# All four projections of the attention layer by seven half-size products, with half the buffers

## The chip, the cores and the metric

The kernel runs on one NeuronCore of one Trainium2 chip. The metric is the device time of one execution in microseconds (us), the median of several runs. In the profile the engines are PE (TensorE, matrix products), DVE (VectorE), ACT (ScalarE), POOL (GpSimd) and SP (SyncE, which here only issues transfers). Each has its own instruction stream, worked off in order; they meet through semaphores.

## The reference, cut to what matters

Two layers over 640 rows of 1024 numbers: 512 rows of a prompt and 8 x 16 rows of samples. Layer 0 is a gated MLP, layer 1 an attention. All data are float32.

```
proj = h @ w_in                       # layer 1: (640 x 1024) @ (1024 x 8208)
q, k, v, z = proj[:, 0:2048], proj[:, 2048:4096], proj[:, 4096:6144], proj[:, 6144:8192]   # 16 heads of 128
logf = log_sigmoid(proj[:, 8192:] + b_f)
# prompt, per head:  p = softmax(q k^T / sqrt(128) + c_i - c_j, causal),  c = cumsum(logf)
# samples: the same over 256 cached rows and the 16 new ones (cache_fox_k, cache_fox_v)
op = (p @ v * silu(z)) @ w_out
x = x + rms_norm(op);  x = x + sigmoid(x @ ple_w_gate) * (p @ ple_w_proj)
```

k and v of the new rows are outputs too.

## The kernel before

**Precision.** Every large float32 product is three products of rounded halves: `split` (lines 270 to 273) has ScalarE write the rounded half `hi` and VectorE the rest `lo = src - hi`, and `mm3` (lines 256 to 260) multiplies hi by hi, hi by lo and lo by hi into the same PSUM bank. A weight is fetched into RAW (three buffers of 512 KB), split into W, and then used; `prefetch` does this as far ahead as W has free places, and `fetch` issues the transfers.

**Layer 0** already makes its u and z projections by `seven_products` (line 533): the four quarters of a product of 256 x 1024 by 1024 x 640 come from seven products of half the size in each direction (Winograd's form of Strassen's scheme) instead of eight. It needs sums of the quarters of the weight, which POOL makes from RAW into a tile `sf` (`left_operands`, line 200), and sums of the quarters of h, which `right_operands` makes once on VectorE and ScalarE into a tile `tb` (lines 409 to 417). Each product covers 4 steps of 128 over the contraction, so 12 matmuls of 320 columns; ScalarE and VectorE add the results up (lines 540 to 555).

**Layer 1** runs over eight pairs of heads. For each pair, `project_v`, `project_k`, `project_q` and `project_z` make 256 columns of the projection. k, q and z come out with heads on partitions (`channel_steps`, line 316): for each of 2 heads and 8 steps three matmuls of 384 columns (`mm3`), one of 512 (line 324) and one of 256 (line 325). v comes out with rows on partitions: for 5 row tiles and 8 steps one matmul of 512 (line 867) and one of 256 columns (line 868). While pair p+1 is projected, the attention of pair p is worked in between: the prompt's scores in four blocks per head, and the samples in two groups of four. Keys of the cache are loaded with the transposition half done and turned by VectorE (line 1018).

**What sets the order.** `interleave` takes a generator of projection steps, each of which yields its time in us, and a list of (time, piece): a piece of the attention is issued when the steps' sum has passed its time. A scheduler then puts the instructions of all engines in a final order by a timeline of its own. All transfers stand in SP's stream, in order (line 119). PSUM has eight banks: 0 to 3 for projections, 4 to 6 for the attention in turn, 7 for the prompt's output.

Of the kernel before, what the change touches and what calls it, by code (L numbers as in the profile page):

```python
# [24 lines left out]
P = 128  # L25
# [32 lines left out]
def hybrid_trunk(tc, x_prompt, x_sample, ck, cv, clf, p_prompt, p_sample, norm_pre, norm_post,  # L58
# [4 lines left out]
    N_SMALL = 288  # L63
    N_R1 = 17664
# [89 lines left out]
    joined = set()  # L154
    for p in range(8):
        for part in (2, 1, 0, 3):
            for kk in range(2):
                if part == 2:
                    joined.add(len(units))
                u_rows(f_win[0], kk * 512, part * E + p * 256, 4, 256)  # L160
# [6 lines left out]
    for i in range(len(units)):  # L167
        if not S0 <= i < S1:
# [4 lines left out]
    n0 = S1 + 16 + 2 + 8  # L173
    few = range(n0, n0 + 64 + 12)
# [28 lines left out]
    def prefetch(upto, i0=0):  # L203

        while len(place) < min(upto, len(items)):
# [64 lines left out]
    def split(hi, lo, src):  # L270

        nc.scalar.activation(out=hi, in_=src, func=AF.Copy)  # L272
        nc.vector.tensor_tensor(out=lo, in0=src, in1=f(hi), op=ALU.subtract)  # L273
# [41 lines left out]

    h_both = A.rearrange("p (z k n) -> p z k n", z=2, k=8)

    def channel_steps(ws, hh, banks):

        out = [bank(banks), bank(banks)]  # L320
        for k in range(8):
            w = [z[:, k % 4, hh * P:(hh + 1) * P] for z in ws[k // 4]]
            mm3(out[0][:, :SA], w, h_at(k, 0, SA), k == 0, k == 7)
            nc.tensor.matmul(out[1].rearrange("p (z n) -> p z n", z=2), w[0], h_both[:, :, k, SA:], start=k == 0, stop=False)  # L324
            nc.tensor.matmul(out[1][:, :TOK - SA], w[1], h_hi[:, k, SA:], start=False, stop=k == 7)  # L325
            yield 0.88
        return out
# [79 lines left out]
    b11, b12, b21, b22, t_a, t_b = (r1(10240 + z * 1280, 1280).rearrange("p (k n) -> p k n", k=4) for z in (0, 1, 2, 3, 4, 0))  # L407

    def right_operands():

# [3 lines left out]
        for o, a, b, dst in ((t_a, b12, b11, 0), (t_b, b22, t_a, 1), (b21, b21, t_b, 2), (b12, b22, b12, None)):  # L414
            nc.vector.tensor_tensor(out=o, in0=a, in1=b, op=ALU.subtract)
# [755 lines left out]
```

## Time and profile before

| | |
|---|---|
| median of 3 runs | 1315.37 us (1315.07 to 1315.51) |
| the profiled execution: its own time | 1315.17 us |
| its span, first to last instruction | 1313.4 us |
| PE busy | 1304.7 us (99%) |
| DVE, ACT, POOL busy | 794.1, 553.1, 136.1 us |
| layer 0, u and z projections | about 150 to 345 us of the span |
| layer 1, its projections begin | at about 531 us |
| layer 1, pairs 1 to 6 beside the attention of 0 to 5 | about 603 to 1042 us, 73 us each |
| output product and tail | from about 1110 us |

A row of an engine's timeline gives start and duration of an instruction. Matmuls are pipelined: a row's duration is longer than the distance to the next row, and it is the distance that costs time. PEld is PE's loading of weights, which runs beside the products. In a row of instruction groups the last number ahead of the bar's second half is the mean duration in ns.

### The profile page before, as it was taken

To read this page: it belongs to the slowest core of one execution; us is meant where nothing else is said; L and a number is where in the kernel's file an instruction comes from. 1 tells how busy PE (TensorE), PEld (TensorE's weight loads), DVE (VectorE), ACT (ScalarE), POOL (GpSimd) and SP (SyncE) were. 2 spreads that over 40 slices of the span, in tenths; PEclk is the share of its full clock that TensorE was granted. 3 is DMA by queue.
4 is the path that set the end of the run, shared out by engine and by line. 5 is a ranking of instruction groups with operands and counts; after the bars stand their busy time and mean duration, and the time that the engine had idled before them with its cause. 6 is when DMAs were issued, how large, how long until landed. Compare 5 with 4: busy or idle time off the path is not lost.

```text
span 1313.4 us, 20355 instructions
## 1 busy us (share of the span) xinstructions
PE 1304.7 (99%) x7683; PEld 1152.3 (88%) x7683; DVE 794.1 (60%) x1671; ACT 553.1 (42%) x1074; POOL 136.1 (10%) x144
## 2 busy tenths in 40 slices
PE   8999999999999999999999999999999999999998
PEld 6888999999988888888999889898988988888887
DVE  7744999999844455644555554556555566554543
ACT  5334555444535343533433334333434344435431
POOL 1012454543000000000000000000000000000100
PEclk8999999999999999999999999999999999999999
DMA  6432333232424213589676665788557687343211
GB/s 227 132 108 67 120 118 121 86 104 73 129 94 149 79 49 113 167 135 149 152 194 151 155 160 148 165 150 171 132 150 163 149 213 235 113 132 132 66 56 57
DMA packets 300053, 172.79 MB, mean 132 GB/s; under 512 B 188785, under 2 KB 269473, under 8 KB 299954
## 3 DMA queue, kind: packets, MB, share of 16 engines
q1 hardware_dynamic: 299810, 171.23, 49.3%
q8 instruction: 60, 0.98, 0.3%
q14 instruction: 39, 0.32, 0.1%
q10 hardware_dynamic: 144, 0.26, 0.1%
HBM read 149.86 MB, written 21.59 MB: 131 GB/s over the span
## 4 chain that ended last, share of the span: by engine, by line
PE 95%; DVE 3%; DMA 1%; issue 1%; ACT 0%; SPq 0%; POOL 0%; DVEq 0%
PE pb L258 22%; PE pb L260 22%; PE pb L259 22%; PE pb L324 7%; PE pb L867 6%; PE pb L325 3%; PE pb L868 3%; PE pb L986 3%; PE pb L979 1%; PE pb L1040 1%; PE pb L1066 1%; PE pb L296 1%; DVE W L273 1%; PE pb L571 1%; PE pb L1063 1%
## 5 line engine op out<-in xcount | busy, mean ns | idle before, releaser
L273 DVE TENSOR_TENSOR W<-RAW,W 128x1024 fp32r<-128x1024 f32 (+1 forms) x156 | 193.5, 1242 | 170.8 <-ACT W L272 136.5
L272 ACT ACTIVATE W<-RAW 128x1024 fp32r<-128x1024 f32 (+1 forms) x156 | 161.0, 1033 | 151.0 <-PE pb L260 47.5
L258 PE MATMUL pb<-A,W 128*128 128x384 f32 (+1 forms) x640 | 221.8, 347 | 0.0
L260 PE MATMUL pb<-A,W 128*128 128x384 f32 (+1 forms) x640 | 208.7, 326 | 0.0
L259 PE MATMUL pb<-A,W 128*128 128x384 f32 (+1 forms) x640 | 208.3, 325 | 0.0
L258 PE MATMUL pb<-W,A 128*128 128x512 f32 x520 | 205.0, 395 | 2.3 <-ACT A L272 2.3
L259 PE MATMUL pb<-W,A 128*128 128x512 f32 x520 | 203.7, 392 | 0.0
L260 PE MATMUL pb<-W,A 128*128 128x512 f32 x520 | 203.3, 393 | 0.1
L324 PE MATMUL pb<-A,W 128*128 128x512 f32 x384 | 150.7, 393 | 0.0
L258 PEld LDWEIGHTS pb<-A,W 128*128 128x128 f32 x640 | 120.4, 188 | 18.7 <-issue 8.9
L259 PEld LDWEIGHTS pb<-A,W 128*128 128x128 f32 x640 | 121.0, 189 | 0.7
L260 PEld LDWEIGHTS pb<-A,W 128*128 128x128 f32 x640 | 120.2, 188 | 0.1
L258 PEld LDWEIGHTS pb<-W,A 128*128 128x128 f32 x520 | 98.1, 189 | 22.3 <-ACT A L272 2.5
L867 PE MATMUL pb<-W,A 128*128 128x512 f32 x320 | 116.6, 403 | 0.0
L260 PEld LDWEIGHTS pb<-W,A 128*128 128x128 f32 x520 | 97.9, 188 | 20.9 <-DVE A L273 0.6
L259 PEld LDWEIGHTS pb<-W,A 128*128 128x128 f32 x520 | 98.0, 188 | 19.4
L325 PE MATMUL pb<-A,W 128*128 128x256 f32 x384 | 107.7, 280 | 0.0
L868 PE MATMUL pb<-W,A 128*128 128x256 f32 x320 | 89.5, 280 | 0.0
L273 DVE TENSOR_TENSOR A<-R,A 128x640 fp32r<-128x640 f32 (+1 forms) x51 | 41.0, 836 | 71.4 <-ACT A L272 70.7
L867 PEld LDWEIGHTS pb<-W,A 128*128 128x128 f32 x320 | 60.0, 188 | 15.1 <-DVE R L872 2.6
L325 PEld LDWEIGHTS pb<-A,W 128*128 128x128 f32 x384 | 72.1, 188 | 0.4 <-issue 0.4
L324 PEld LDWEIGHTS pb<-A,W 128*128 128x128 f32 x384 | 72.1, 188 | 0.2
(252 smaller groups left out, 2285.8 us busy)
## 6 DMA issues: line engine op xcount, KB each, us to landing
RAW<-in_fox_w_in SPq DMA_DIRECT2D x64, 512.0 KB
RAW<-in_gmlp_w_in SPq DMA_DIRECT2D x40, 512.0 KB
r2b_t<-in_cache_fox_v SPq DMA_DIRECT2D x32, 512.0 KB
r2b_t<-in_cache_fox_k SPq DMA_DIRECT2D x128, 128.0 KB
RAW<-in_gmlp_w_out SPq DMA_DIRECT2D x16, 512.0 KB
RAW<-in_ple_w_gate SPq DMA_DIRECT2D x16, 512.0 KB
RAW<-in_fox_w_out SPq DMA_DIRECT2D x16, 512.0 KB
out<-R SPq DMA_DIRECT2D x42, 128.0 KB
```

The source lines that it names most:

```text
L258: nc.tensor.matmul(out, lh, rh, start=start, stop=False)
L259: nc.tensor.matmul(out, lh, rl, start=False, stop=False)
L260: nc.tensor.matmul(out, ll, rh, start=False, stop=stop)
L272: nc.scalar.activation(out=hi, in_=src, func=AF.Copy)
L273: nc.vector.tensor_tensor(out=lo, in0=src, in1=f(hi), op=ALU.subtract)
L296: nc.tensor.transpose(out=b[:, j * P:(j + 1) * P], in_=src[:, (4 * c + j) * P:(4 * c + j + 1) * P], identity=ident)
L324: nc.tensor.matmul(out[1].rearrange("p (z n) -> p z n", z=2), w[0], h_both[:, :, k, SA:], start=k == 0, stop=False)
L325: nc.tensor.matmul(out[1][:, :TOK - SA], w[1], h_hi[:, k, SA:], start=False, stop=k == 7)
L571: nc.tensor.matmul(b0[:, t * P:(t + 1) * P], v_at(pnl, t)[:, c0:c0 + P], wm, start=True, stop=True)
L867: nc.tensor.matmul(b, hi, w, start=k == 0, stop=False)
L868: nc.tensor.matmul(b[:, :256], lo, w[:, :256], start=False, stop=k == 7)
L986: nc.tensor.matmul(O[:, d], v[:, j, hh * P:(hh + 1) * P], pt[:, j * P:(j + 1) * P], start=(j == 0), stop=(j == i))
```

## The change

- `project_k`, `project_q`, `project_z` and, from pair 1 on, `project_v` call `seven_products`. Only pair 0's v is made as before. `seven_products` now yields after every three matmuls.
- v then has heads on partitions as the others do; `turn_v` has TensorE transpose it (10 transposes of 128 x 128 per pair) and ScalarE copy it out of PSUM.
- The sums of the quarters of h are made once more at the start of layer 1 (`right_operands`), and one quarter of h is overwritten with a difference.
- The sums of the weights' quarters are made on POOL for every projection; the factor of q goes into the split of its weights.
- The tiles for the sums take 10240 columns, so R1 (17760 columns) holds the rest: z, q, k and the cached V have one buffer each, the cached K half of one, y is written over z. K is loaded head by head. In the attention W has 8 places of 1024 columns as before.
- The masked bias of the prompt's diagonal block is made per block by POOL (128 columns) instead of per head by VectorE (512 columns).
- z of pair p is now projected in the pass that works the attention of pair p, ahead of v, k, q of pair p+1; the times of the pieces are new.

```diff
-            z = i % NRAW if i < S0 else (i + 1) % NRAW
...
+    S2 = len(units)
+    joined, scaled = {S2, S2 + 1}, set()
+    for part, p in [(2, 0), (1, 0), (0, 0)] + [x for p in range(8) for x in ((3, p), (2, p + 1), (1, p + 1), (0, p + 1)) if x[1] < 8]:
...
-        if not S0 <= i < S1:
+        if not (S0 <= i < S1 or S2 + 2 <= i < S3):
             items.append((i, None))
         elif i % 2 == 0:
             items += [(i, j) for j in range(4)]
...
                 if u > S0:
-                    fetch(u + 4)
+                    fetch(u + 4 + (u > S1 and j == 3))
...
+    o_KT, o_K, o_V, o_q, o_k, o_vk = 0, 2176, 3200, 5248, 6528, 7808
+    o_u, o_P, o_PT, o_v, o_qp = 9088, 9728, 10752, 11776, 14336
+    o_Ws, o_Ps, o_PTs, o_W0, o_z = 14848, 15120, 15520, 15904, 16480
...
+    def turn_v(p, i):
+        v = v_of(p)
+        b = bank(ATT)
+        for t in range(4):
+            nc.tensor.transpose(out=b[:, t * P:(t + 1) * P], in_=both(o_vk, i)[:, t * P:(t + 1) * P], identity=ident)
+        nc.scalar.activation(out=v[:, :4, i * P:(i + 1) * P], in_=b.rearrange("p (t n) -> p t n", t=4), func=AF.Copy)
+        if i:
+            b = bank(ATT)
+            for z in range(2):
+                nc.tensor.transpose(out=b[:, z * P:(z + 1) * P], in_=both(o_vk, z)[:, 512:], identity=ident)
+            nc.scalar.activation(out=v[:, 4], in_=b[:, :256], func=AF.Copy)
+            for t in range(NT):
+                store_v(p, t)
+
+    def project_v(p):
+        yield from seven_products(lambda i, j: both(o_vk, i)[:, HALF[j]], lambda i, j, c: None)
...
     def project_k(p):
-        ws = weights(2)
...
+        def done(i, j, c):
+            if (i, j) not in ((0, 0), (1, 0)):
+                return
+            h = 2 * p + i
+            tr = both(o_vk, i)
+            nc.vector.transpose(out=tr, in_=both(o_k, i))
...
+        yield from seven_products(lambda i, j: both(o_k, i)[:, HALF[j]], done)
...
     def project_z(p):
-        ws = weights(2)
...
+        def done(i, j, c):
+            th = r1(o_vk + ring("th", (0, 1)) * HT, HT)
+            nc.scalar.activation(out=th, in_=c, func=AF.Tanh, scale=0.5)
+            nc.vector.scalar_tensor_tensor(out=c, in0=th, scalar=1.0, in1=c, op0=ALU.add, op1=ALU.mult)
...
         def scores(i):
+            w1 = w1_at()
+            nc.gpsimd.tensor_tensor(out=w1, in0=w0[:, d], in1=causal, op=ALU.add)
...
+    interleave(project_v0(), [(0.0, forget_logits), (0.1, sums_of_h), (6.0, log_forget)])
+    split(*quarter(0, 1), sums[0])
...
     for p in range(7):
...
+        pieces = attention_pieces(p, 4.8, 24.7) + next_keys(p + 1, 28.0, 39.5)
+        pieces += [(26.0, lambda p=p: turn_v(p + 1, 0)), (27.0, lambda p=p: turn_v(p + 1, 1))]
+        interleave(project(project_z(p), project_v(p + 1), project_k(p + 1), project_q(p + 1)), pieces)
         store_y(p)
...
     interleave(project_z(7), [x for x in pieces if x[0] <= now])
+    pool2.release()
+    pool2, R2 = second("r2c", F32)
+    load_y(range(2, 14))
```

The lines of the changed kernel are numbered anew: 262 to 264 are `mm3`, 280 the `lo` of a split, 410 and 412 the sums of h's quarters, 539 to 555 the additions of `seven_products`, 871 and 872 the two matmuls of v for pair 0. `tbf` and `sff` are the tiles of the sums in layer 1, `A` holds h, `R_69` is R1.

**Place 1: VectorE at the start of layer 1**, from the last split of h (`A<-pb`). Before:

```order
L273 TENSOR_TENSOR A<-pb_77,A 128x4x128
L273 TENSOR_TENSOR A<-pb_75,A 128x4x128
L872 TENSOR_TENSOR R_69<-R_69,pb_73 128x256
L273 TENSOR_TENSOR W<-RAW,W 128x1024 x2
L872 TENSOR_TENSOR R_69<-R_69,pb_70 128x256
L794 COPY r2b_t<-pb_76 128x160
```

Now:

```order
L280 TENSOR_TENSOR A<-pb_77,A 128x4x128
L280 TENSOR_TENSOR A<-pb_75,A 128x4x128
L410 TENSOR_TENSOR R_69<-A 128x1280 x2
L876 TENSOR_TENSOR R_69<-R_69,pb_73 128x256
L412 TENSOR_TENSOR R_69<-R_69 128x1280 x3
L280 TENSOR_TENSOR W<-sff,W 128x1024
L280 TENSOR_TENSOR tbf<-R_69,tbf 128x1280
L412 TENSOR_TENSOR R_69<-R_69 128x1280
L802 COPY R_69<-pb_76 128x160
L280 TENSOR_TENSOR W<-RAW,W 128x1024
L876 TENSOR_TENSOR R_69<-R_69,pb_70 128x256
L280 TENSOR_TENSOR tbf<-R_69,tbf 128x1280
```

The additions and splits of 1280 columns are new; two of the four additions L410 stand ahead of these rows.

**Place 2: TensorE at the same time**, the end of pair 0's v (lines 867, 868 before) and the first products of k. Before:

```order
L867 MATMUL pb_70<-W,A 128x512
L868 MATMUL pb_70<-W,A 128x256
L324 MATMUL pb_72<-A,W 128x512
L325 MATMUL pb_72<-A,W 128x256
L259 MATMUL pb_71<-A,W 128x384
L260 MATMUL pb_71<-A,W 128x384
```

Now:

```order
L871 MATMUL pb_70<-W,A 128x512
L872 MATMUL pb_70<-W,A 128x256
L262 MATMUL pb_71<-A,W 128x320
L263 MATMUL pb_71<-A,W 128x320
L801 MATMUL pb_76<-CST,R_69 128x32 x2
L829 MATMUL pb_75<-CST,R_69 128x272
L830 MATMUL pb_75<-CST,R_69 128x144
L262 MATMUL pb_72<-tbf,W 128x320
L264 MATMUL pb_71<-A,W 128x320
```

The rows on `pb_71` are k's fifth product (quarter 1,1 of h), which the scheduler has put ahead of the second; `pb_72<-tbf` is the first matmul on a sum of quarters. Ten more rows of `pb_71` follow, then the first of `pb_73`, on the overwritten quarter of h.

**Place 3: SP's stream around the stores of the turned k** (`out<-R_69 32x...`, eight transfers per head). Before:

```order
L119 DMA out<-R_69 32x16x32
L119 DMA out<-R_69 32x4x32
L119 DMA RAW<-in_fox_w_in 128x4x256 x2
L119 DMA r2b_t<-in_cache_fox_k 32x32x32 x4
L119 DMA R_69<-cs_sc 128x1x272
L119 DMA r2b_t<-in_cache_fox_k 32x32x32
```

Now:

```order
L121 DMA out<-R_69 32x16x32
L121 DMA out<-R_69 32x4x32
L121 DMA RAW<-in_fox_w_in 128x4x256 x2
L121 DMA R_69<-in_cache_fox_v 128x4x256 x2
L121 DMA y_sc<-R_69 128x640
L121 DMA CST<-c_sc 128x512
```

The two forms of store alternate, and only their last two are shown in each case: before, the eight stores of one head stand ahead of two weight loads (and the other head's eight stand further down); now all sixteen of a pair stand together ahead of two weight loads, and four loads of cached keys and five stores of v ahead of the sixteen.

More of the change, by code (lines that the diff above doesn't have):

```diff
@@ L62, in hybrid_trunk @@
     NRAW, NW = 3, 5
[L63 to L64 removed]
+    N_SMALL, N_KEPT = 192, 172
+    N_R1 = 17760
     N_WARM = 3
@@ L104, in bank @@
         return PB[ring(("bank", lst), lst)]
+    kept_end = N_KEPT
     def small(n=1, keep=False):
-        name, first, end = ("kept", 0, 172) if keep else ("small", 172, N_SMALL)
+        name, first, end = ("kept", 0, N_KEPT) if keep else ("small", kept_end, N_SMALL)
         i = counters.get(name, first)
@@ L153, in hybrid_trunk @@
     u_tail(g_wout, 0)
[L154 to L160, printed above, removed]
+    S2 = len(units)
+    joined, scaled = {S2, S2 + 1}, set()
+    for part, p in [(2, 0), (1, 0), (0, 0)] + [x for p in range(8) for x in ((3, p), (2, p + 1), (1, p + 1), (0, p + 1)) if x[1] < 8]:
+        if part == 0:
+            scaled.add(len(units))
+        for kk in range(2):
+            u_rows(f_win[0], kk * 512, part * E + p * 256, 4, 256)
+    S3 = len(units)
     u_tail(f_wout, 1)
@@ L314, in hybrid_trunk @@
     SPLITS = ((0, SA), (SA, TOK))
[L316 to L327, printed above, removed]
     def run(steps):
@@ L455, in hybrid_trunk @@
                 with queued("act", "dve"):
-                    right_operands()
+                    b12 = right_operands([10240 + z * 1280 for z in range(5)])
             if (p, kk) == (3, 1):
@@ L930, in prompt_pieces, with project, load_w0 @@
+    def project(*parts):
+        for part in parts:
+            yield from part
+    W0 = [r1(o_W0, 512), tri]
+    w1_at = lambda: SF[:, 2368:2368 + P]
+    def load_w0(h):
+        dma(W0[h % 2], c_sc[h].partition_broadcast(P))
     def prompt_pieces(h):
@@ L1019, in turn_k, with load_v, new_k @@
+    def load_v(p, bg):
+        for z in range(2):
+            b = 4 * bg + 2 * z
+            dma(vv[:, 2 * z:2 * z + 2].rearrange("p b t n -> p (b t) n"),
+                cv[0, b:b + 2, :, 2 * p:2 * p + 2, :].rearrange("b (t k) h d -> k (b t) (h d)", k=P))
+    def turn_k(p, bg, hh):
+        for bl in range(4):
+            nc.vector.transpose(out=kt[:, hh, bl, :PAST], in_=kraw[:, bl])
+    def new_k(p, bg):
+        for hh in range(2):
             nc.gpsimd.tensor_copy(out=kt[:, hh, :, PAST:], in_=kn_of(2 * p + hh)[:, 64 * bg:64 * bg + 64].rearrange("p (b k) -> p b k", b=4))
@@ L1084, in prompt_times @@
     def prompt_times(h, t0, step):
-        load, setup, scores, turn, values = prompt_pieces(h)
-        res = [(t0 - 12, load), (t0 - step + 0.1, setup)]
+        setup, scores, turn, values = prompt_pieces(h)
+        res = [(t0 - step + 0.1, setup)]
         for i in range(4):
@@ L1102, in store_y, with load_y @@
             dma(y_sc[2 * p + hh], y_of(2 * p + hh))
+    def load_y(heads):
+        for g in heads:
+            dma(y_again(g, 0), y_sc[g])
     def y_again(g, half):
@@ L1107, in y_again @@
             return y_of(g)
-        if half == 0 and 7 <= g < 11:
-            return f(A[:, 7680 + (g - 7) * TOK:7680 + (g - 6) * TOK])
-        return r1(g * TOK, TOK) if g < 7 else r2((g - 7) * TOK, TOK)
-    def load_y(heads, half):
-        for g in heads:
-            dma(y_again(g, half), y_sc[g])
-    PARTS = (project_v, project_k, project_q, project_z)
-    interleave(project(0, PARTS), [(0.0, forget_logits), (6.0, log_forget), (20.0, forget_sums), (30.0, lambda: load_k(0, 0))])
-    for p in range(7):
-        length, step = (57, 5.6) if p < 6 else (43, 4.2)
-        pieces = kv_times(p, 0, 5) + kv_times(p, 1, length / 2) + sample_times(p, 0, 5) + sample_times(p, 1, length / 2)
-        pieces += [(2, lambda p=p: load_k(p, 1)), (length / 2 - 3, lambda p=p: load_k(p + 1, 0))]
-        for hh in range(2):
-            pieces += prompt_times(2 * p + hh, 2 + 4 * step * hh, step)
-        interleave(project(p + 1, PARTS if p < 6 else PARTS[:3]), pieces)
-        store_y(p)
@@ L1135, in hybrid_trunk @@
+    load_y(range(2))
+    now = 12.35
+    pieces = attention_pieces(7, 5.2, 24.7)
     interleave(project_z(7), [x for x in pieces if x[0] <= now])
+    pool2.release()
+    pool2, R2 = second("r2c", F32)
+    load_y(range(2, 14))
+    w1_at = lambda: r2(9840, P)
     ATT = (5, 6)
```

210 lines of the change are left out of this document (90 added, 120 removed).

## The prediction, made before the changed kernel was run

> **What bounds the kernel now.** I read the page's head, the chain of waits, then the busy time by stretches for one pair of layer 1 and one pair of layer 0, where the same seven products are already in use.
>
> ```profile
> PE 1304.7 (99%) x7683; PEld 1152.3 (88%) x7683; DVE 794.1 (60%) x1671; ACT 553.1 (42%) x1074; POOL 136.1 (10%) x144
> PE 95%; DVE 3%; DMA 1%; issue 1%; ACT 0%; SPq 0%; POOL 0%; DVEq 0%
> 750.00:822.92 72.92, 72.92 (x484) 65.32 (x480) 39.39 (x121) 28.51 (x68) 1.96 (x6) 1.00 0.61 155
> 262.25:289.55 27.30, 27.30 (x194) 27.28 (x193) 25.17 (x39) 12.68 (x24) 12.79 (x9) 1.00 0.31 93
> ```
>
> The columns of the last two rows are length, then busy time of PE, PEld, DVE, ACT and POOL, granted clock, DMA share and GB/s. PE has no idle time in either stretch, at the full clock: 72.92 us per pair of heads in layer 1, 27.30 us for two seven-product projections with their gating in layer 0. So time goes down only by what PE no longer has to do, as long as nobody makes PE wait. The second row also gives the limit to watch: in layer 0 VectorE is busy 25.17 of 27.30 us (92%) and PE still never waits; in layer 1 VectorE has 39.39 of 72.92 (54%).
>
> **The change part by part. 1: PE's products.** The distances between rows of PE's timeline:
>
> ```profile
> 809.90 0.34 PE L258 MATMUL pb<-A,W 128*128 128x384 f32 x1
> 810.77 0.34 PE L258 MATMUL pb<-A,W 128*128 128x384 f32 x1
> 536.82 0.39 PE L867 MATMUL pb<-W,A 128*128 128x512 f32 x1
> 538.90 0.39 PE L867 MATMUL pb<-W,A 128*128 128x512 f32 x1
> 264.77 0.31 PE L260 MATMUL pb<-A,W 128*128 128x320 f32 x1
> 269.17 0.31 PE L260 MATMUL pb<-A,W 128*128 128x320 f32 x1
> 632.79 0.44 PE pb L979 x4
> ```
>
> One step of k, q or z (three matmuls of 384 columns, one of 512, one of 256) takes 0.87 us; 16 steps make 13.9 us. Six steps of v lie between the next two rows, 0.347 us each; 40 make 13.9 us. Thirty matmuls of 320 columns lie between the two rows of layer 0: 0.1467 us each, and a projection by seven products has 7 x 12 = 84 of them, 12.3 us. That saves 1.55 us on each of 24 projections of k, q and z, and as much on 7 of v (pair 0's v stays): 31 x 1.55 = 48.1 us. Against this v must be turned: four transposes take 0.44 us in the chain, ten take 1.1 us, and I add 0.3 us for three more changes between kinds of matmul (in the following rows a first matmul after another kind is 0.26 us ahead of its successor, in place of 0.18).
>
> ```profile
> 807.63 0.42 PE L258 MATMUL pb<-A,W 128*128 128x384 f32 x1
> 807.89 0.34 PE L259 MATMUL pb<-A,W 128*128 128x384 f32 x1
> 808.07 0.34 PE L260 MATMUL pb<-A,W 128*128 128x384 f32 x1
> ```
>
> Seven pairs make 9.8 us. Net, PE loses 48.1 - 9.8 = 38.3 us; a pair goes from 72.9 to 72.9 - 4 x 1.55 + 1.4 = 68.1 us. The attention's own products are the same in number and shape.
>
> **2: VectorE in the loop.** Per pair it loses eight splits of 1024 columns, the five additions of v, those of q, k and z, and the bias of 512 columns; it gains twelve splits of 1024 and four of 512, seven additions of 320 columns for each of four projections, and four multiplications for z.
>
> ```profile
> L273 DVE TENSOR_TENSOR W<-RAW,W 128x1024 fp32r<-128x1024 f32 x74 | 90.4, 1224 | 104.8 <-ACT W L272 72.2 <-PE pb L325 25.4 <-PE pb L868 3.7
> L273 DVE TENSOR_TENSOR W<-R,W 128x512 fp32r<-128x512 f32 x32 | 21.5, 688 | 1.0 <-ACT W L272 1.0
> L872 DVE TENSOR_TENSOR R<-R,pb 128x256 f32<-128x256 f32 x39 | 16.3, 418 | 21.1 <-ACT R L871 21.1
> L540 DVE TENSOR_TENSOR R<-R,pb 128x320 f32<-128x320 f32 x55 | 25.2, 479 | 1.7 <-PE pb L260 0.9
> L589 DVE SCALAR_TENSOR_TENSOR R<-R 128x320 f32<-128x320 f32 x12 | 5.9, 490 | 0.8
> L513 DVE TENSOR_TENSOR R<-CST,R 128x128 f32<-128x128 f32 x14 | 11.5, 821 | 0.0
> L1050 DVE TENSOR_TENSOR R<-CST,R 128x128 f32<-128x128 f32 x16 | 4.4, 273 | 0.0
> ```
>
> Gained: 12 x 1.224 + 4 x 0.688 + 28 x 0.479 + 4 x 0.490 = 32.8 us. Lost: 8 x 1.224 for splits, 5 x 0.418 for v, and for the drains of k, q and z and the bias about 14 more additions near 0.4 us, an estimate from L872: 17.5 us. So 39.4 + 32.8 - 17.5 = 54.7 of 68.1 us (80%). The last two rows show what comes on top. The same kind of addition with the same operands' shape takes 821 ns in layer 0, where POOL sums the weights, and 273 ns in the loop, where POOL is nearly idle.
>
> ```profile
> L200 POOL TENSOR_TENSOR sf<-R,RAW 128x512 f32<-128x512 f32 x6 | 7.8, 1302 | 13.8 <-DVE W L273 13.8
> L200 POOL TENSOR_TENSOR sf<-RAW,sf 128x512 f32<-128x512 f32 x12 | 23.5, 1962 | 0.9
> L1033 POOL TENSOR_TENSOR R<-R,CST 128x16 f32<-128x16 f32 x16 | 4.3, 267 | 164.6 <-DMA R<-cs_sc 164.6
> ```
>
> POOL gets 16 sums of 512 columns (1.30 to 1.96 us) and 8 bias blocks of 128 columns per pair; between 16 columns at 0.27 and 512 at 1.30 us a block is about 0.5. That is 25 to 35 us of 68. If each sum costs VectorE as much waiting as those 821 - 273 = 0.55 us, VectorE gets 16 x 0.55 = 9 us more: 64 of 68 us, 94%, where layer 0 stands at 92% without harm. I take 0 to 4 us of PE idle per pair as the bounds and 0.6 as my value, 4 us for seven pairs, nearer to layer 0's zero, since VectorE's rows in the loop have more to wait for. ACT has room: 28.5 us now, and even 20 more instructions of the size of a large split (1.06 us) leave it at 50.
>
> The Trainium skill has a rule against this change ("SBUF — State Buffer", Who interferes with whom): a VectorE instruction with two inputs in SBUF and a GpSimd instruction that reads SBUF shut each other out for a whole instruction. The rows of 821 and 273 ns agree. By that rule the shared time here, some 30 us of POOL and 20 of VectorE's splits and gates, still fits in 68.
>
> **3: The start of layer 1.** The sums of h's quarters now stand between the last rows of h and k's products.
>
> ```profile
> 545.03 1.29 DVE L273 TENSOR_TENSOR A<-pb,A 128x512 fp32r<-128x512 f32 x2 [0.23 <-ACT A L272]
> L415 DVE TENSOR_TENSOR R<-R 128x1280 f32<-128x1280 f32 x4 | 5.9, 1486 | 0.0
> L272 ACT ACTIVATE tb<-R 128x1280 fp32r<-128x1280 f32 x3 | 3.8, 1280 | 5.3 <-DVE R L415 5.3
> 552.99 0.28 PE L868 MATMUL pb<-W,A 128*128 128x256 f32 x1
> ```
>
> h is complete at 546.3. Of VectorE's eight additions two are ahead; the order shown above has five of 1.49 us and one of 0.42 to come before the sum that k's second product needs: 546.3 + 7.9 = 554.2, and ScalarE's rounding (1.28) makes 555.5. The difference that overwrites a quarter of h comes after one split of 1.22 and two more rows of 1.49: 558.4, rounded at 559.7. PE meanwhile has v (done at about 553.2 before, with eight matmuls of k, 1.4 us, already in between) and k's first product (1.76 us), so it is free at about 553.9. It waits 1.6 us for the first, does ten matmuls of k's fifth product (1.5 us) and waits 2.7 us for the second. That is 4 us; POOL's sums for q fall into the same time, so I take 5. The bounds are 0 (h is complete earlier, since its rows are worked off in another order now) and 15 (VectorE's whole row of eleven instructions of 1.49 us after h, less 1.76).
>
> **4: Buffers and the end.** z is written over by the next pair only at its fourth product, 7 us into the pass; the store of y, issued at the end of the pass before, has that long. At the end, twelve heads of y are loaded only after the last z (before: half of them during it), with one step of the output product and the two heads already there as cover; I take 1 us, bounds 0 and 5.
>
> The sum, against the profiled execution's own 1315.2 us, which lies 0.2 below the median: 1315.2 - 38.3 + 4 + 5 + 1 = 1286.9. I say **1287 us**.
>
> **The rivals.** *The start costs its upper bound and the loop loses 2 us per pair:* 15 + 14 + 1 in place of 10, 1307 us. For it speaks VectorE at 94%, with chains of small steps (maximum, exponent, reciprocal) between the splits; against it, layer 0.
>
> *Slower: weight loads behind the stores of k.* In SP's stream all sixteen stores of a pair now stand ahead of two weight loads.
>
> ```profile
> L119 SPq DMA_DIRECT2D out<-R x16: 349/444/513, 772.7 to 793.7; - x16
> L119 SPq DMA_DIRECT2D r2b_t<-in_cache_fox_k x8: 328/559/3412, 783.7 to 795.3; - x8
> 764.00:766.00 2.00, 2.00 (x12) 1.61 (x10) 0.58 (x2) 0.06 (x1) 0.00 (x0) 1.00 0.92 305
> ```
>
> Sixteen issues at 0.444 us are 7.1 us, and 512 KB at the 305 GB/s of the third row 1.7 more: about 9 us, which the projections' four PSUM banks cover (four products of 1.76 us stretched by the attention's share, 68.1/49.3, are 9.7 us). But a load of cached keys has stood up to 3.4 us in issue, and four such stand just ahead. With all four at that, 13.6 us more, ScalarE stands before the next split and PE waits 9 + 13.6 - 9.7 = 13 us per pair: 1287 + 7 x 12.4 = 1374. It costs the whole gain from (38.3 - 6)/7 = 4.6 us of PE idle per pair on; then the kernel is slower. Against it: VectorE's and ScalarE's splits run more than one projection ahead of PE, and such stores cost PE nothing before.
>
> *Slower: VectorE is shut out by POOL.* If every sum and block on POOL held VectorE for its whole length (16 x 1.30 + 8 x 0.5 = 25 us), VectorE would need 54.7 + 25 = 80 us per pair, 7 more than now: 1315 + 7 x 7 + 6 = 1370. This would be the Trainium skill's rule above at its worst. From 54.7 + 18.2 us on it is no gain. Layer 0 speaks against it: there 8 sums lie in 27.3 us, here 16 in 68.
>
> **How the numbers follow.** Forecast 0.66 (its own range 1277 to 1299), first rival 0.17, loads behind stores 0.10, VectorE shut out 0.04, all else 0.03. The range reaches from the sum without any idle, 1315.2 - 38.3 = 1277, less 2 for what PE's rows round away, to just above the first rival: 1275 to 1309. 0.2% (2.6 us) is about what a measurement of this kernel can tell. Faster: the forecast and the first rival, 0.83. Slower: 0.14. Between: 0.03, where the idle happens to eat the gain.
>
> **What would show it.** Right: pairs repeat every 68 to 69 us with PE busy throughout; VectorE is busy 58 to 64 us of it, POOL 25 to 35; matmuls of 320 columns in layer 1 stand 0.147 us apart; one gap of PE of about 5 us soon after the last split of h, released by ScalarE or VectorE on the sums. Wrong: a period over 70 us, with PE waiting for splits of W whose ScalarE rows wait for RAW (second rival) or whose VectorE rows last far over 1.22 us (third); or a gap of 10 us and more at the start of layer 1.

## The result: 7% slower, and the profile after

The changed kernel takes 1410.5 us in the median (1407.6 to 1415.9), against 1315.4 us for the kernel before on the same chip: a ratio of 1.0728 (95% interval 1.0691 to 1.0766). Forecast were 1287 us, at most 1309. The profiled execution took 1413.1 us, with a span of 1411.3 us.

The head of the page of the changed kernel, its row of the granted clock in 40 slices, and the chain of work that ended last, by engine:

```profile
PE 1316.6 (93%) x7877; PEld 1169.1 (83%) x7877; DVE 946.7 (67%) x1815; ACT 586.6 (42%) x1061; POOL 354.9 (25%) x332
PEclk9999999999999999999899999898998999999999
PE 64%; DVE 14%; DMA 12%; SPq 4%; issue 4%; ACT 1%; POOL 0%; DVEq 0%; ACTq 0%; POOLq 0%
```

PE was 99% busy before and made up 95% of the chain. Now DMA has 12% of the chain and VectorE 14%, and the clock is under 0.9 in several slices of layer 1 (the second half of the span). The waits of the changed kernel say for what (total us, times, longest):

```profile
ACT W L279 <- DMA RAW<-in_fox_w_in: 144.7, 23, 11.2
ACT W L282 <- DMA RAW<-in_fox_w_in: 49.6, 8, 9.2
DVE W L280 <- ACT W L279: 163.1, 71, 9.3
DVE R L1016 <- DMA R<-in_cache_fox_k: 27.7, 6, 10.3
PE pb L962 <- DVE SML L971: 23.1, 7, 5.6
PE pb L262 <- DVE R L555: 21.4, 6, 6.5
PE pb L262 <- DVE R L552: 13.1, 7, 5.0
```

ScalarE stands 194 us for weights of layer 1 that have not landed, before it can round them (lines 279 and 282), and VectorE stands behind ScalarE. In the kernel before, the same wait was this:

```profile
ACT W L272 <- DMA RAW<-in_fox_w_in: 7.2, 2, 4.8
```

The last three rows above are the surprising ones. PE does not wait for split weights (`W`). It waits for VectorE's additions of finished products (`R`, lines 552 and 555) and for a maximum of the scores (line 971), that is, for PSUM banks that VectorE has not emptied. One such place, from the timeline of the changed kernel (start, duration, engine, line, operation; in brackets the idle time just before and what ended it):

```profile
853.12 1.71 DVE L280 TENSOR_TENSOR W<-RAW,W 128x1024 fp32r<-128x1024 f32 x1
...
858.26 1.22 DVE L280 TENSOR_TENSOR W<-sff,W 128x1024 fp32r<-128x1024 f32 x1
862.95 1.28 DVE L280 TENSOR_TENSOR W<-RAW,W 128x512 fp32r<-128x512 f32 x1 [3.47 <-ACT W L279]
...
864.62 0.47 DVE L555 TENSOR_TENSOR R<-R,pb 128x320 f32<-128x320 f32 x1
...
855.85 0.43 SPq L121 DMA_DIRECT2D RAW<-in_fox_w_in  x1
...
862.29 0.63 ACT L279 ACTIVATE W<-RAW 128x512 fp32r<-128x512 f32 x1 [5.19 <-DMA RAW<-in_fox_w_in]
...
862.97 0.31 PE L264 MATMUL pb<-tbf,W 128*128 128x320 f32 x1
865.14 0.42 PE L262 MATMUL pb<-A,W 128*128 128x320 f32 x1 [1.87 <-DVE R L555]
```

RAW has three buffers, and a projection by seven products takes two of them: the first is held until POOL has made its sums, the second until the projection's last split (128 x 1024). That split ends on VectorE at 854.8; only then can SP request the first weights of the projection after next (855.85). The scheduler has put the first split of just those weights (128 x 512) close behind, ahead of two splits of the next projection, whose weights are already there. ScalarE can start 6.4 us after the request, and has stood 5.2 us; VectorE stands 3.5 us, and the addition of line 555, for which everything is ready, stands behind them. PE needs that split only much later, but the addition now.

The second part of the loss stands right behind the gap. The two rows are stretches of PE around and behind the restart (length, busy us of PE, PEld, DVE, ACT, POOL, granted clock, DMA share, GB/s):

```profile
863.00:865.00 2.00, 0.28 (x2) 0.01 (x1) 2.00 (x4) 1.54 (x4) 0.69 (x1) 1.00 0.75 155
866.00:869.40 3.40, 3.40 (x15) 3.31 (x14) 3.40 (x7) 1.92 (x5) 3.27 (x4) 0.51 0.00 0
```

And the matmuls of 320 columns ahead of the gap and behind it:

```profile
860.07 0.31 PE L263 MATMUL pb<-A,W 128*128 128x320 f32 x1
860.22 0.31 PE L264 MATMUL pb<-A,W 128*128 128x320 f32 x1
...
866.58 0.47 PE L262 MATMUL pb<-A,W 128*128 128x320 f32 x1
866.84 0.47 PE L263 MATMUL pb<-A,W 128*128 128x320 f32 x1
```

Ahead of the gap they stand 0.147 us apart, behind it 0.267. For about 3.3 us after the gap PE is "busy" at half speed. The Trainium skill ("TensorE: Matmul & The Clock Gate", Part 1: The HAM clock gate) describes such a half rate, set in windows of some 3.4 us; the trace agrees with that. Its table "Why this matters for your kernels" gives idle gaps of about 3 us as what brings the rate down; here a gap of 1.87 us was enough, though behind another of 1.89 us, at 601.7, the clock stayed full.

Idle time and clock together give the loss of a pass. A pass is counted from the first gating of one pair's z (ScalarE's row of line 924, here 864.85) to that of the next (950.95):

```profile
864.90:951.00 86.10, 75.12 (x506) 68.63 (x506) 56.40 (x139) 32.13 (x67) 28.93 (x30) 0.92 0.58 130
```

PE is idle for 86.1 - 75.1 = 11.0 us, and a clock of 0.92 costs 0.08 x 86.1 = 6.9 us more: 17.9 us, of 18.6 that this pass takes over the 67.5 us of the experiment that comes first below.

### The profile page after: what moved, and what is told of

The parts are those of the page before. It is cut to its first block, busy times and chain, and to the rows that moved or that the text cites. A ratio compares the mean times of both kernels' runs of the same rounds, so it can differ in the third digit from the quotient of the medians.

```text
span 1411.3 us, 21215 instructions
## 1 busy us (share of the span) xinstructions
PE 1316.6 (93%) x7877; PEld 1169.1 (83%) x7877; DVE 946.7 (67%) x1815; ACT 586.6 (42%) x1061; POOL 354.9 (25%) x332
## 4 chain that ended last, share of the span: by engine, by line
PE 64%; DVE 14%; DMA 12%; SPq 4%; issue 4%; ACT 1%; POOL 0%; DVEq 0%; ACTq 0%; POOLq 0%
PE pb L262 19%; PE pb L263 19%; PE pb L264 19%; DMA RAW<-in_fox_w_in 5%; SPq L121 4%; DMA R<-in_cache_fox_k 4%; DVE W L280 3%; DVE R L1016 2%; DMA R<-c_sc 2%; DVE R L539 1%; PE pb L991 1%; DMA R<-in_cache_fox_v 1%; PE pb L571 1%; PE pb L1064 1%; PE pb L306 1%
## 5 line engine op out<-in xcount | busy, mean ns | idle before, releaser
L262 PE MATMUL pb<-A,W 128*128 128x320 f32 x752 | 248.8, 331 | 21.4 <-DVE R L555 21.4
L264 PE MATMUL pb<-A,W 128*128 128x320 f32 x752 | 237.8, 316 | 0.0
L263 PE MATMUL pb<-A,W 128*128 128x320 f32 x752 | 237.8, 316 | 0.0
L279 ACT ACTIVATE W<-RAW 128x1024 fp32r<-128x1024 f32 (+1 forms) x140 | 134.2, 959 | 228.6 <-DMA RAW<-in_fox_w_in 144.7
L262 PE MATMUL pb<-W,A 128*128 128x512 f32 x520 | 204.6, 394 | 1.5 <-ACT A L279 1.5
L263 PE MATMUL pb<-W,A 128*128 128x512 f32 x520 | 203.7, 392 | 0.0
L264 PE MATMUL pb<-W,A 128*128 128x512 f32 x520 | 203.2, 393 | 0.2 <-DVE A L280 0.2
L262 PEld LDWEIGHTS pb<-A,W 128*128 128x128 f32 x752 | 145.7, 194 | 31.0 <-DVE R L555 23.0
L203 POOL TENSOR_TENSOR sff<-RAW 128x512 f32<-128x512 f32 x62 | 84.2, 1359 | 260.6 <-DMA RAW<-in_fox_w_in 188.1
L263 PEld LDWEIGHTS pb<-A,W 128*128 128x128 f32 x752 | 146.0, 194 | 1.7 <-issue 1.3
L264 PEld LDWEIGHTS pb<-A,W 128*128 128x128 f32 x752 | 145.6, 194 | 0.5 <-issue 0.4
L262 PE MATMUL pb<-tbf,W 128*128 128x320 f32 x372 | 126.9, 341 | 18.4 <-DVE R L552 12.8
L264 PE MATMUL pb<-tbf,W 128*128 128x320 f32 x372 | 120.3, 323 | 0.0
L263 PE MATMUL pb<-tbf,W 128*128 128x320 f32 x372 | 120.0, 323 | 0.0
L262 PEld LDWEIGHTS pb<-W,A 128*128 128x128 f32 x520 | 98.1, 189 | 21.0 <-ACT A L279 1.9
L264 PEld LDWEIGHTS pb<-W,A 128*128 128x128 f32 x520 | 98.0, 188 | 20.7 <-DVE A L280 0.7
L263 PEld LDWEIGHTS pb<-W,A 128*128 128x128 f32 x520 | 98.0, 188 | 19.6
L262 PEld LDWEIGHTS pb<-tbf,W 128*128 128x128 f32 x372 | 74.8, 201 | 26.7 <-DVE R L552 13.6
L975 ACT ACTIVATE R<-R,SML 128x128 f32<-128x128 f32 (+1 forms) x64 | 35.9, 561 | 115.8 <-DVE SML L974 115.7
L1016 DVE STREAM_TRANSPOSE R<-R 128x256 f32<-128x256 f32 x128 | 47.6, 415 | 45.8 <-DMA R<-in_cache_fox_k 27.7
```

What stands on the lines that cost most here:

```text
L203: nc.gpsimd.tensor_tensor(out=o, in0=a, in1=b, op=op)
L262: nc.tensor.matmul(out, lh, rh, start=start, stop=False)
L263: nc.tensor.matmul(out, lh, rl, start=False, stop=False)
L264: nc.tensor.matmul(out, ll, rh, start=False, stop=stop)
L975: nc.scalar.activation(out=pr[:, :n], in_=pr[:, :n], func=AF.Exp, bias=nm, accum_out=sm)
L1016: nc.vector.transpose(out=kt[:, hh, bl, :PAST], in_=kraw[:, bl])
```

## The experiments

Line numbers differ between the kernels: the splits' lines 279, 280 and 282 here are 283, 284 and 286 from f_order on, and 1016, the turn of cached keys, is 1021 or 1022. Passes are those of pairs 0 to 6, counted as above. Where no interval is given, one execution was timed beside one of the kernel before. The four executions of the changed kernel lie 8 us apart, those of h_first 6.5, so smaller differences between single executions tell nothing.

| kernel | us | passes of pairs 0 to 6, us |
|---|---|---|
| changed kernel | 1410.5 | 88.1, 88.6, 78.8, 86.1, 90.8, 89.4, 74.1 |
| d_weights | 1287.3 | 70.4, 67.5, 67.5, 67.5, 67.5, 67.5, 69.2 |
| d_cache | 1352.4 | 82.8, 77.7, 73.2, 73.4, 80.9, 81.3, 67.3 |
| d_sums | 1359.4 | 83.6, 78.8, 74.7, 77.6, 80.8, 79.7, 70.6 |
| d_stores | 1411.4 | 87.5, 88.6, 79.8, 84.7, 90.3, 88.5, 75.8 |
| f_order | 1342.3 | 79.1, 77.4, 72.0, 73.6, 74.0, 79.8, 71.4 |
| f_cache | 1300.0 | 74.7, 68.1, 68.1, 68.1, 68.1, 68.1, 68.6 |
| f_keys_pin | 1379.3 | 85.4, 86.9, 72.9, 77.6, 82.1, 85.2, 74.4 |
| g_kact | 1355.6 | 96.9, 74.9, 71.0, 73.1, 78.3, 75.8, 70.3 |
| g_kpool | 1340.8 | 94.9, 70.7, 69.2, 71.4, 75.9, 79.3, 70.8 |
| g_wact | 1336.3 | 79.5, 76.2, 69.4, 70.2, 77.1, 72.0, 71.3 |
| h_three_only | 1361.5 | 83.6, 80.6, 73.2, 76.9, 83.3, 79.1, 69.4 |
| h_three | 1319.9 | 89.0, 68.7, 67.4, 67.5, 70.3, 75.7, 68.8 |
| h_keys | 1314.8 | 92.0, 72.1, 67.5, 67.5, 69.0, 69.9, 68.8 |
| h_first | 1307.1 | 75.3, 69.1, 67.5, 67.8, 67.2, 69.8, 68.7 |

### Four suspects, each taken away alone

**d_weights: the weight loads of layer 1 left out** from pair 0's z on (stale weights are split in their place).

```diff
-            dma(raw_of(state["raw"]).rearrange("p (k n) -> p k n", k=k), ap)
+            if not S2 + 6 <= state["raw"] < S3:
+                dma(raw_of(state["raw"]).rearrange("p (k n) -> p k n", k=k), ap)
```

> Leaves out the weight loads of layer 1 from pair 0's z on; the splits then work on what lies in RAW, so the outputs of the attention layer are other numbers. Theory (ScalarE and VectorE stand in order before splits whose weights have not landed, and PE runs dry behind them): nearly all of the loop's loss goes, time 1285 to 1310 us. Rival (VectorE and POOL shut each other out, or VectorE is simply full): no load was the matter, time stays above 1370 us.

Measured: 1287.3 us. The first row is the pass of pair 2, the second the loop's first 546 us:

```profile
741.00:808.50 67.50, 67.50 (x508) 63.66 (x508) 57.91 (x139) 32.55 (x67) 29.44 (x31) 1.00 0.45 104
600.00:1146.00 546.00, 546.00 (x3946) 503.94 (x3946) 449.15 (x1081) 263.63 (x521) 205.31 (x216) 1.00 0.49 123
```

PE has no idle time in the loop, at the full clock, though VectorE and POOL do all their work. So the products, the turning of v, the additions and the contention of VectorE with POOL keep PE waiting nowhere in the loop, and all of the loss hangs on the weight loads. This run does not separate their landing from their traffic and from what their requests hold up behind them in SP's stream: f_order, below, hardly waits for weights any more and is still 55 us above this time. In the changed kernel the same 546 us read so:

```profile
600.00:1146.00 546.00, 472.16 (x3192) 426.96 (x3191) 362.13 (x889) 205.19 (x413) 189.09 (x194) 0.93 0.58 132
```

PE is busy for 86.5% of them at a clock of 0.93, which makes 0.80 of the work; its matmuls are 3192 of 3946, 0.81.

**d_cache: the loads of cached keys and values left out**, all but the first.

```diff
     def load_k(p, bg, hh):
+        if (p, bg) > (0, 0) or hh:
+            return
```

(and the same in `load_v` without `hh`)

> Leaves out all loads of cached K and V but the first, so the sample outputs are other numbers; weight loads and POOL's sums stay. If the transfers' traffic as a whole makes the weights late, they land in 4 us or so in place of 7 and the time falls by half the loss or more, to 1300 to 1350 us. If only the order of request and split makes them late, half of the waits for RAW stay and only the waits for keys go: 1360 to 1390 us. If VectorE and POOL are the cause: above 1390 us.

Measured: 1352.4 us, just above the one range and below the other. ScalarE still stands for weights:

```profile
ACT W L279 <- DMA RAW<-in_fox_w_in: 120.0, 23, 9.1
ACT W L282 <- DMA RAW<-in_fox_w_in: 20.5, 8, 4.3
```

Without 32 MB of traffic and its issues on SP, 141 of 194 us of these waits stay. The cached loads add to the lateness (58 us of time are gone, and with them the waits for keys); they are not its only cause.

**d_sums: POOL's sums of weights left out** in layer 1, all but the first.

```diff
-        if j == 0:
+        if j == 0 and i < S2 + 4:
```

> Leaves out POOL's sums of the weights' quarters in layer 1 but the first, so the projections are other numbers; loads, splits and the products' number stay. Rival (POOL shuts VectorE out): time falls to 1320 us or below. Theory (late transfers): VectorE's rows get shorter, the waits for RAW stay in kind, 1360 to 1410 us.

Measured: 1359.4 us, just under the range that the theory gave. The waits, and POOL's busy time (its last column ahead of the clock) in the loop:

```profile
ACT W L279 <- DMA RAW<-in_fox_w_in: 139.4, 23, 10.9
ACT W L282 <- DMA RAW<-in_fox_w_in: 35.9, 8, 5.9
...
600.00:1146.00 546.00, 500.52 (x3534) 456.19 (x3536) 360.72 (x966) 225.90 (x454) 46.23 (x100) 0.97 0.63 147
```

With POOL busy for 46 us in place of 189 ScalarE still stands 175 us for weights, so VectorE shut out by POOL is not what makes the weights late. What the 51 us are that it gained was not separated. One way stands in the waits of SP in the changed kernel: a buffer of RAW is free only when POOL has summed it.

```profile
SPq L121 <- POOL sff L203: 92.5, 17, 7.6
```

**d_stores: the sixteen stores of k per pair left out**, for pairs 1 to 7. These are the ones that the prediction's second rival put ahead of the weight loads.

```diff
-            for qd in range(4):
+            for qd in range(4 if p == 0 else 0):
```

> The changed kernel without the stores of k of pairs 1 to 7 (16 stores per pair left out; the splits stand where the scheduler put them). If the sixteen stores ahead of two weight loads are what makes the weights late (the rival of the prediction, word for word): one late split of four per pair goes, and the keys behind them: under 1360 us. If every first split of a projection stands too close behind its load (theory): three or four late splits of a pair stay, 1370 to 1400 us.

Measured: 1411.4 us, as if nothing had been left out. My own theory missed too, since it gave them at least 10 us. The stores from pair 1 on do not make the weights late; those of pair 0 were left in.

### The order of the splits

**f_order: the splits of layer 1 held in the order in which they are written**, on ScalarE and VectorE; nothing is left out.

```diff
-                split(*(...), left_operands(u, j), scale if u in scaled else None)
+                left = left_operands(u, j)
+                with queued(*(("act", "dve") if u > S2 + 4 else ())):
+                    last = split(*(...), left, scale if u in scaled else None)
+                if u > S2:
+                    behind["act"], behind["dve"] = last
...
+        return a, d
```

> Same work as the changed kernel; only the splits of the seven-product weights in layer 1 are held in the written order on ScalarE and VectorE, so that the first split of a projection stands behind the last of the one before, some 20 to 30 VectorE rows later than the scheduler had put it. Theory: the weights then have landed when their split comes up, the waits for RAW fall from 190 us on ScalarE to under 60, time 1310 to 1350 us, and what is left are waits for cached keys. Rival (traffic, or VectorE and POOL): the order changes little, above 1390 us.

What it moves, from VectorE's final order (row number, line, operation, operands; only the splits of RAW and of POOL's sums `sff`), first in the changed kernel, then in f_order:

```
706 L280 TENSOR_TENSOR W<-RAW,W 128x1024
718 L280 TENSOR_TENSOR W<-sff,W 128x1024
719 L280 TENSOR_TENSOR W<-RAW,W 128x512
728 L280 TENSOR_TENSOR W<-sff,W 128x1024
740 L280 TENSOR_TENSOR W<-RAW,W 128x1024
```

```
707 L284 TENSOR_TENSOR W<-RAW,W 128x1024
708 L284 TENSOR_TENSOR W<-RAW,W 128x512
720 L284 TENSOR_TENSOR W<-sff,W 128x1024
732 L284 TENSOR_TENSOR W<-sff,W 128x1024
740 L284 TENSOR_TENSOR W<-RAW,W 128x1024
742 L284 TENSOR_TENSOR W<-RAW,W 128x512
```

The last split of one projection (128 x 1024 of RAW, row 706 or 707) lets the first weights of the projection after next be requested. Their split (128 x 512) is 13 rows behind in the changed kernel, and 35 rows in f_order. By the traces it is 13 to 15 rows throughout the loop from its second projection on, and 22 to 43 in f_order.

Measured: 1342.3 us. Its waits:

```profile
ACT W L283 <- DMA RAW<-in_fox_w_in: 6.7, 4, 3.1
DVE R L1021 <- DMA R<-in_cache_fox_k: 55.9, 13, 8.3
```

ScalarE's 194 us of standing for weights are down to 10 (6.7 here and 3.0 at line 286), and 68 us of time are gone. Yet the weights land no sooner: 7.7 us in the median from request to landing, against 7.3 in the changed kernel, by their pages. These medians rest on the 10 and 8 of 64 loads whose landing the page can tell. Worked out for all 64 from the traces (the last landing signal on a load's semaphore ahead of the semaphore's next request), the median is 7.0 us in f_order, 6.8 in the changed kernel and 6.1 in the kernel before. So the order took ScalarE's waits away, without any faster transfer. What stands now is VectorE, for the cached keys, which have one buffer of half the size: a load must wait for the turn of the one before, and in VectorE's order two of the four turns of a pair are only 20 and 21 rows behind the one before.

**f_cache: f_order without the cached loads** but the first, to see if that is all that is left.

> f_order without the loads of cached keys and values after the first (stale keys and values are used; the traffic of 32 MB less). Theory (after the splits of the weights are in written order, only the cached keys are late): PE's gaps in the loop fall under 10 us in all, 1288 to 1300 us. Rival (VectorE's own work beside POOL keeps PE waiting, or the weights are still late): 1315 and more.

Measured: 1300.0 us, at the upper end. PE is idle for 3 of the loop's 546 us:

```profile
600.00:1146.00 546.00, 542.82 (x3876) 494.99 (x3875) 456.48 (x1074) 260.73 (x510) 214.45 (x220) 0.99 0.43 115
```

**f_keys_pin: f_order with the turns of cached keys held in their places on VectorE too**, and written further behind their loads.

```diff
-            nc.vector.transpose(out=kt[:, hh, bl, :PAST], in_=kraw[:, bl])
+            with queued(*(("dve",) if bl == 0 and p + bg > 0 else ())):
+                behind["dve"] = nc.vector.transpose(out=kt[:, hh, bl, :PAST], in_=kraw[:, bl])
...
-            pieces += [(s0 + 12.1, lambda: load_k(p + 1, 0, 0)), ...
+            pieces += [(s0 + 13.5, lambda: load_k(p + 1, 0, 0)), ...
-        pieces = attention_pieces(p, 4.8, 24.7) + next_keys(p + 1, 28.0, 39.5)
+        pieces = attention_pieces(p, 4.8, 24.7) + next_keys(p + 1, 30.0, 42.1, 12)
```

> The splits of the weights in written order as in f_order, and now the turns of the cached keys too: each turn stands on VectorE where it is written, behind the splits written ahead of it, and is written 12 to 13 of a pass's 49 units after its load in place of 9 to 11. Theory (VectorE was put in front of transfers that had not landed): of the 55.9 us in which VectorE stood for cached keys in f_order most goes, and with it PE's gaps ahead of the values of the next head: 1300 to 1325 us. Rival (the queue on SP and its traffic are late as such, whatever the order on VectorE): no better than f_order, 1335 to 1350.

Measured: 1379.3 us, a miss by more than 50 us to the wrong side. The wait of VectorE, and a row of SP's timeline:

```profile
DVE R L1022 <- DMA R<-in_cache_fox_k: 90.2, 22, 9.0
...
836.18 9.77 SPq L121 DMA_DIRECT2D R<-in_cache_fox_k  x4
```

I had moved a load of keys behind two loads of V, and there its four issues alone took 9.8 us of SP, with everything behind them late. With keys, weights and stores in one stream, moving one of them made others late.

### The one stream

Three kernels take something out of SP's stream, all on top of f_order: **g_kact** requests the cached keys from ScalarE, **g_kpool** from POOL, **g_wact** requests the weights of the loop from ScalarE.

```diff
# g_kact; g_kpool has nc.gpsimd in place of nc.scalar
-            dma(kraw[d].rearrange("p b (c d) -> p (b c) d", d=32),
-                ck[0, 4 * bg:4 * bg + 4, ...
+            nc.scalar.dma_start(out=kraw[d].rearrange("p b (c d) -> p (b c) d", d=32),
+                in_=ck[0, 4 * bg:4 * bg + 4, ...
# g_wact
-            dma(raw_of(state["raw"]).rearrange("p (k n) -> p k n", k=k), ap)
+            (nc.scalar.dma_start if S2 + 8 <= state["raw"] < S3 else dma)(out=raw_of(...)..., in_=ap)
```

> f_order with the loads of cached keys issued by ScalarE's queue in place of SP's (same bytes, same pieces). Theory (one stream: in f_order SP stands before a load of keys until VectorE has turned the last ones, and for 2 to 9 us in its issue, and the weights' requests stand behind, and the other way round): the waits of VectorE for cached keys fall from 55.9 us to under 25, and the time to 1300 to 1325 us, unless ScalarE, which then waits for the turns, is late with splits. Rival (the transfers themselves are too slow for 20 rows of VectorE between request and turn): 1335 and more.

> The same with the loads of cached keys issued by POOL. Theory: SP's stream is free of them, 1300 to 1325 us. Rival: POOL is too late with them behind its sums of weights, or they take longer to issue there, 1335 and more.

> f_order with the weights of the loop requested by ScalarE's queue, all else on SP. Theory (one stream): the median from request to landing of these weights falls from 7.7 us to under 5, SP's waits for the split of W go, and the keys' requests are earlier: 1305 to 1330 us. Rival (ScalarE then stands for VectorE's last split and POOL's sums before each request, and what is queued behind it, splits and exponents, is late): 1340 and more.

Measured: 1355.6, 1340.8 and 1336.3 us, none as good as the theory had it. g_kact shows the price that the expectation named: VectorE stands only 3.3 us for keys, but ScalarE stands in their place.

```profile
ACT R L1071 <- DMA R<-in_cache_fox_k: 13.1, 1, 13.1
ACT W L283 <- DMA R<-in_cache_fox_k: 10.4, 1, 10.4
```

g_kpool and g_wact differ by 1.5 and 6 us from f_order, which single executions cannot tell apart, but the passes differ by more: the pass of pair 0 is 16 us longer in g_kpool, and most later passes are shorter in both. So two more: **h_three** with both (keys by POOL, weights by ScalarE) on top of f_order, and **h_three_only** with both but without f_order's edit.

> f_order with both: the weights of the loop requested by ScalarE, the cached keys by POOL, all else by SP; each gave 2 to 6 us alone. Theory (what is left in f_order is requests that stand behind each other): the gains add up and PE's idle time in the loop falls under 20 us, 1300 to 1325 us. Rival (what is left is VectorE, which stands in order for keys that land 5 us after a request whatever the queue): no better than the best of the two, 1330 to 1342.

> The changed kernel with these three queues and nothing else: the splits stand where the scheduler puts them. Theory (the place of the first splits is the cause, the queue only adds to it): ScalarE still stands for RAW in most projections, 1370 to 1410 us. Rival (the weights are late since their requests stand on SP): near h_three, under 1345.

Measured: 1319.9 and 1361.5 us. In h_three the theory held. In h_three_only neither did: the queues alone took back 49 us, order alone 68, both 91. ScalarE's wait in h_three_only says why the queues cannot do it alone:

```profile
ACT W L279 <- DMA RAW<-in_fox_w_in: 106.6, 23, 10.4
```

The Trainium skill ("DMA: Bandwidth & Descriptors", Issuing engines are not separate DMA queues) says that requests from several engines only save the time in which an engine issues them, which it calls usually small. The runs agree as far as landing tells: worked out as above for all 64 weight loads, its median is 6.5 us in h_three_only against 6.8 in the changed kernel, and 6.7 in h_three against 7.0 in f_order. But where requests stand in order behind the waits of other requests, separate streams were worth 22 us (f_order to h_three).

### What was left, and a version that beats both

**h_keys** is h_three with the edit of f_keys_pin, which now has no loads of V ahead of the keys: the turns are 29 to 38 rows of VectorE apart, where they were 23 to 48 by turns.

> h_three with the turns of the cached keys held on VectorE at the places and times of f_keys_pin: 29 to 38 rows of VectorE between one turn and the next, in place of 23 to 48 by turns. Theory (what is left are keys that land after VectorE's turn of them; f_keys_pin was slower only since its loads of keys stood behind those of V on SP): VectorE's waits for cached keys fall from 29 us to under 10, 1295 to 1312 us, less than before the change. Rival (something that neither order nor queue mends): 1318 and more.

Measured: 1314.8 us, a ratio to the kernel before of 0.9997 (0.9987 to 1.0007): no difference, and between theory and rival. VectorE's wait for keys went from 29.1 to 18.9 us, not under 10. The passes show where the rest is: pairs 2 to 6 take 67.5 to 69.9 us, near the floor, but pair 0 takes 92.0.

**h_first** is h_keys with the keys of pair 0 requested by SP.

```diff
-            nc.gpsimd.dma_start(out=kraw[d]...
+            (nc.gpsimd if p else nc.sync).dma_start(out=kraw[d]...
```

> h_keys with the cached keys of pair 0 alone requested by SP, as in f_order, where the pass of pair 0 takes 79 us in place of 92. Theory (what is left in h_keys is the start: the first keys stand behind POOL's sums): the pass of pair 0 falls to 76 to 84 us and the time to 1301 to 1309 us. Rival (the start is late for another reason, the masks and stores around it): 1313 and more.

Measured: 1307.1 us, 0.9949 of the kernel before (0.993 to 0.9968), so half a per cent faster, with the pass of pair 0 at 75.3 us. First a stretch of its loop, then a row of SP in it:

```profile
760.00:850.00 90.00, 90.00 (x682) 84.22 (x681) 82.31 (x184) 45.13 (x90) 56.37 (x61) 1.00 0.59 160
...
853.04 24.75 SPq L121 DMA_DIRECT2D out<-R  x21
```

PE is busy throughout, with VectorE at 91%. And the row of the 21 stores of a pair spans 24.8 us of SP, 12.4 of them waits (6.7 for VectorE's turn of k, 5.7 for earlier loads to land). The pass in which they lie, that of pair 3, takes 67.8 us all the same: neither weights nor keys are queued behind them.

## Why the prediction was wrong, point by point

- **Part 1, PE's products: right.** 68.1 us per pair were forecast, 67.5 measured where nothing is late. That d_weights, the kernel without its late weights, meets the forecast to 0.4 us is luck in part: the sum had 5 us for waits at the start, 4 in the loop and 1 at the end, and d_weights loses 11 at the start (rows below) and none in the other two.
- **Part 2, VectorE in the loop: this step failed.** The work was right: 54.7 us and up to 9 for POOL were summed, d_weights has 57.9 in a pass, and PE did not wait at 86%. The term of 0.6 us of PE idle per pair, with bounds of 0 and 4, was wrong, since it came from how much VectorE has to do. It is not short of time; it stands in order. In the pass shown, PE idles 11.0 us, and the clock takes 6.9 more, for which the sum had no term at all. "VectorE's rows in the loop have more to wait for" was written down and given 0.6 us.
- **Part 3, the start of layer 1: too low, within its bounds of 0 and 15.** 5 us of idle were forecast; three gaps at the sums make 0.97 + 4.54 + 0.99 = 6.5 us. The largest was not released by a sum, as forecast, but by line 876, VectorE's last addition of v. It empties a PSUM bank, and it stands behind the sums and a split in VectorE's order. The next rows are the whole start in the changed kernel, in d_weights and in the kernel before.

```profile
566.64 0.63 PE L262 MATMUL pb<-tbf,W 128*128 128x320 f32 x1 [4.54 <-DVE R L876]
...
531.00:603.00 72.00, 62.43 (x379) 55.17 (x377) 62.87 (x77) 31.14 (x47) 29.27 (x22) 0.95 0.42 110
531.00:603.00 72.00, 64.61 (x390) 55.93 (x388) 67.93 (x88) 33.19 (x51) 32.88 (x26) 0.95 0.33 87
531.00:603.00 72.00, 72.00 (x422) 63.61 (x422) 33.27 (x67) 25.69 (x48) 2.42 (x6) 1.00 0.77 155
```

PE is idle for 9.6, 7.4 and 0 us of it, and the clock of 0.95, which the sum did not have, takes 0.05 x 72 = 3.6 us more in the first two.

- **Part 4, the end:** 1 us was forecast; neither the changed kernel nor d_weights has a gap of PE over 0.3 us after 1200 us.
- **The second rival, weights late, had the right sign to look for** (a period over 70 us, and ScalarE's rows waiting for RAW) and the wrong mechanism, at a chance of 0.10. Its sixteen stores do nothing from pair 1 on (d_stores). It priced a landing at 1.7 us for 512 KB, from the best rate of a stretch; the changed kernel's page has 7.3 us from request to landing, and 3.5 in layer 0 (for all loads, worked out as above, 6.8 and 4.5):

```profile
RAW<-in_fox_w_in SPq DMA_DIRECT2D x64, 512.0 KB, 7.3
RAW<-in_gmlp_w_in SPq DMA_DIRECT2D x40, 512.0 KB, 3.5
```

- **What was held against that rival was true, but no help:** VectorE's and ScalarE's splits "run more than one projection ahead of PE". They do, and this is the harm: a split that stands far ahead of its use stands as close to its request, with buffers that come free so late, and whatever is queued behind it waits. The cover of four PSUM banks was counted for PE's need of weights; what ran out was the emptying of these banks.
- **The third rival, VectorE shut out by POOL:** d_weights has all of POOL's sums and no idle time of PE. What POOL's sums add to VectorE shows in d_sums, in the pass of pair 3:

```profile
842.90:920.50 77.60, 71.94 (x514) 65.78 (x514) 51.49 (x139) 32.21 (x66) 6.35 (x14) 0.98 0.66 146
```

VectorE is busy for 51.5 us there and for 56.4 in the same pass of the changed kernel, with 139 instructions in each: about 5 us per pair, of the 9 that the prediction added on top. In this loop the rule of the Trainium skill cited there costs VectorE no more, and PE nothing.

Three things stay open. The first is how the 51 us that d_sums gained divide between earlier buffers and VectorE's shorter rows. The second is whether a fourth buffer of RAW, or a whole one for the cached keys, would have done what the order did; no run has more buffers. The third is the 20 us by which h_first stays above d_weights: some 8 of them lie in its passes, nearly 9 ahead of the first, which begins at 611.7 against 603.1. Its trace shows where these arise. The first keys of pair 0 are requested by SP at 596.8, behind 19 stores; VectorE stands 10.8 us for them, PE stands 7.6 us until the first is turned, and then runs at a clock of 0.50 for 10.2 us. Whether the stores hold up that request was not tried.

```profile
607.98 1.43 DVE L1022 STREAM_TRANSPOSE R<-R 128x256 f32<-128x256 f32 x4 [10.79 <-DMA R<-in_cache_fox_k]
```

## What to carry to other kernels

An engine that works in order and has time to spare can still stop the one that bounds: look at what is queued behind each of its instructions that waits for a transfer, and how many rows lie between a request and the first row that needs it. When a change halves buffers or holds them longer, count from the moment at which a buffer comes free to the place of its next reader in the engine's final order, as the scheduler puts it and not as it is written, with the landing time that such loads have in this kernel. And price a gap of PE at more than its length: here 74 us of idle time in the loop came with a clock of 0.93.

## What the runs showed of the hardware that was not expected

- After a gap of 1.87 us PE ran at half its pace for 3.3 us (0.267 us in place of 0.147 for a matmul of 320 columns), while the profile showed it busy. In layer 1 of the changed kernel a stretch at half the granted clock goes with each of the 16 gaps of 1.96 us and more. The length alone does not decide: behind a gap of 1.89 us the clock stayed full, as this row shows, which begins with the gap.

```profile
601.70:609.00 7.30, 5.43 (x29) 3.63 (x30) 4.09 (x12) 3.02 (x5) 2.62 (x5) 1.00 0.99 190
```

- Four loads of cached keys took SP from 2 to 12 us to issue (9.8 in the row of f_keys_pin above), and POOL 3.1 us in each of three rows of g_kpool. One of these rows, and the transfers' row of the page of f_order and of h_first, where POOL issues the keys from pair 1 on:

```profile
707.27 3.11 POOL L1009 DMA_DIRECT2D R<-in_cache_fox_k  x4 [3.01 <-DVE R L1021]
```

```profile
DMA packets 299482, 171.54 MB, mean 128 GB/s; under 512 B 188721, under 2 KB 269409, under 8 KB 299378
```

```profile
DMA packets 188378, 171.54 MB, mean 132 GB/s; under 512 B 74033, under 2 KB 154721, under 8 KB 188274
```

The same bytes went in 111,000 fewer packets, nearly all of them among those under 512 bytes. Whether this is why the issue is steady was not tried.
